# Projection results that ScalarE makes: their stores move from the queue of the loads to ScalarE's own queue

## The chip, the cores and the metric

The kernel runs on one core of a Trainium2 chip. The metric is the device time of one execution in microseconds (us). A core has a matrix engine (PE, with PEld for its weight loads), VectorE (DVE), ScalarE (ACT), GpSimd (POOL) and SyncE (SP). Each engine runs its own list of instructions strictly in order. A DMA (a transfer between the chip's memory and on-chip memory) is issued by an instruction in the list of one engine. In this kernel, before the change, all of them are issued from SP.

## The reference, cut to what matters

One step of a one-layer hybrid decoder for 1024 prompt tokens and 8 sample tokens. The inputs are projected by `w_in` (1024 x 3224), the parts go through four mixers (S5, mLSTM, GLA, RWKV-7), the outputs are joined by `w_out`, and a gated feed-forward network follows.

```python
h = rmsnorm(x, norm_mix)
proj = (h @ w_in).astype(F32)
(u, mq, mk, mv, mi, mf, mo, gq, gk, gv, ga, gg, rcols) = _split(proj, IN_SIZES)
...
mix = jnp.concatenate([y_s5, y_ml, y_gla, y_rw], axis=-1) @ w_out
x = x + mix.astype(x.dtype)
h2 = rmsnorm(x, norm_ffn)
up = (h2 @ ffn_w_up).astype(F32)
...
x = x + ffn.astype(x.dtype)
```

## The kernel before

**Stages.** The 1032 tokens are cut in two segments, `SEGS`: tokens 0 to 511, and tokens 512 to 1031 with the samples. `build` runs: the projection of segment 0, `win(0)`; the mixers for the first quarters of the tokens, `go(SEQ0)`; the projection of segment 1, `win(1)`; `w_out` and the feed-forward network of segment 0; the remaining mixers, `go(SEQ1)`; then `w_out` and the feed-forward network of segment 1. This is the order in which the program is written. On the engines the stages lie over one another: mixer work of segment 0 runs among the projection of segment 1, and so on.

**A projection.** Weights come as 128x1024 tiles of 512 KB (`load_w`, L1121 to L1123): SP issues the load into `wr` (every third one into `p`), ACT rounds it to a high part (`wh`, L1122), POOL makes the low part (`wl`, L1123). `mm3` (L1140 to L1142) multiplies three times for one product: high by high, high by low, low by high. There are two forms of projection:

- `w_in_fm` gives 128 features by the tokens of the segment. For segment 0, VectorE multiplies the result by the row norm (L1221). For segment 1 the inputs are already normed (`hr` is a list and `None`), so ScalarE copies the result out of PSUM (L1220), in two chunks of 260 tokens. One store then writes the tile `t` to a scratch tensor in the chip's memory (L1222): `rcD`, `mlD` or `glD`.
- `w_in_tm` gives tokens by 256 features. ScalarE copies the result out in both segments (L1249), and a store for every 256 tokens (L1250) writes it to `uD`, `gvD` or `mvD`.

The mixers read these scratch tensors back (`rcD` at L144 and L146, `uD` at L778, `glD` at L330, L332 and L364, `mlD` at L509 and L514, `gvD` at L331, `mvD` at L512). So a store here is followed, sooner or later, by a load of the same data from the same queue. The tiles `t` come from a pool of five (`TB`).

**What sets the order.** Nothing is put in order by hand. The recording layer's scheduler places each engine's instructions by a simulated timeline and by priorities: weight and input loads with their splitting have one base number (`S`), the projections and the feed-forward network another (`E`), their matmuls a third (`G`), the mixers follow the program. The result is a fixed list for each engine. A change of one instruction's engine can therefore move others, on all engines.

**Waits.** Each instruction carries the semaphores that it waits for. DMAs that land add to one of eight semaphores, which are dealt out in turn over all DMAs (`DMAHW0` to `DMAHW7`, with a number behind, in the rows below). Before a DMA is issued, its engine waits until the DMA before it on the same semaphore, some eight DMAs earlier in the schedule, has landed. Other waits are for the engine that made the data or that still reads the buffer (`Activation`, `DVE`, `Pool`, `PE`).

Of the kernel before, what the change touches and what calls it, by code (L numbers as in the profile page):

```python
# [1109 lines left out]
def load_w(k,src,tags=None):  # L1110

    nc=k.nc; k.wn+=1
    if tags: r=k.wp.tile([128,1024],F32,tag="wr",name="wr",bufs=k.wb[0]); h,l=[k.ga.tile([128,1024],F32R,tag=n,name=n) for n in tags]
    elif k.w3 and k.wn%3==0: r,h,l=[k.ga.tile([128,1024],t,tag=n,name=n) for n,t in (('p0',F32),('p1',F32R),('p2',F32R))]
    else: r,h,l=[k.wp.tile([128,1024],t,tag=n,name=n,bufs=b) for n,t,b in zip(('wr','wh','wl'),(F32,F32R,F32R),k.wb)]
    shp=src.shape; n=int(np.prod(shp[1:]))
    def view(t):
        v=t[:,0:n]
        return v if len(shp)==2 else v.rearrange("p (a b)->p a b",a=shp[1]) if len(shp)==3 else v.rearrange("p (c a b)->p c a b",c=shp[1],a=shp[2])
    with k.pr('S'):  # L1120
        nc.sync.dma_start(out=view(r),in_=src)  # L1121
        nc.scalar.copy(h[:,0:n],r[:,0:n])  # L1122
        for c in range(0,n,256): nc.gpsimd.tensor_tensor(out=l[:,c:c+256],in0=r[:,c:c+256],in1=h[:,c:c+256].bitcast(F32),op=ALU.subtract)  # L1123
    return view(h),view(l)

def tt(k): return k.tp.tile([128,HW],F32,tag="t",name="t",bufs=k.tb)
def htile(k,i): return k.ga.tile([128,2,HW],F32R,tag="h%d"%i,name="h%d"%i)
def gps(k,tag=None): return k.psm.tile([128,512],F32,tag=tag,name=tag,bufs=1 if tag=="mc" else 2) if tag else k.psg.tile([128,512],F32,tag="g",name="g")
# [5 lines left out]
def mm3(k,out,w,hs,c0,c1):  # L1134

    T=k.nc.tensor; wh,wl=w; n=len(hs)
    with k.pr('G'):
        for i,h in enumerate(hs):
            a=h[:,0,c0:c1]; b=h[:,1,c0:c1]
            T.matmul(out,wh[:,i],a,start=i==0,stop=False)  # L1140
            T.matmul(out,wh[:,i],b,start=False,stop=False)  # L1141
            T.matmul(out,wl[:,i],a,start=False,stop=i==n-1)  # L1142

def chunks(N):
    return [(0,N)] if N<=512 else [(0,N//2),(N//2,N)]
# [64 lines left out]
def w_in_fm(k,hr,seg,idx,w=None,tag=None):  # L1210
    nc=k.nc; c0,c1=seg; N=c1-c0; hs,r=hr
    w=w or load_w(k,k.wfm[idx])
    dst,sc=k.fmdst[idx]
    e=tt(k); ps=[]
    for a,b in chunks(N):
        p=gps(k,tag); ps.append(p)
        mm3(k,p[:,0:b-a],w,hs,a,b)
    if r is not None: r=r.rstd()
    for (a,b),p in zip(chunks(N),ps):
        if r is None: nc.scalar.activation(out=e[:,a:b],in_=p[:,0:b-a],func=AF.Identity,scale=sc)  # L1220
        else: nc.vector.scalar_tensor_tensor(out=e[:,a:b],in0=p[:,0:b-a],scalar=sc,in1=r[:,a:b],op0=ALU.mult,op1=ALU.mult)  # L1221
    nc.sync.dma_start(out=dst[:,c0:c1],in_=e[:,0:N])  # L1222

def w_in_tm(k,hr,seg,which):

    nc=k.nc; T=nc.tensor; V=nc.vector; A=nc.scalar; c0,c1=seg; N=c1-c0; hs,r=hr
    src=dict(mv=k.wmv,gv=k.wgv,u=k.wu)[which]; dst=dict(mv=k.mvD,gv=k.gvD,u=k.uD)[which]
    n=N//128; m=N%128
    ps=[]; q=None
    for pi in range(2):  # L1230
        wh,wl=load_w(k,src[pi])
        with k.pr('G'):
            for i in range(n):
                if pi==0 and i%2==0: ps.append(gps(k))
                o=ps[i//2][:,i%2*256:i%2*256+256]
                for kk in range(4):
                    h=hs[pi*4+kk]; a=h[:,0,i*128:i*128+128]; b=h[:,1,i*128:i*128+128]
                    z=T.matmul(o,a,wh[:,kk],start=pi==0 and kk==0 and i%2==0,stop=False)  # L1238
                    if pi==0 and kk==0 and i%2: k.tc.keep_in_program_order(z)
                    T.matmul(o,a,wl[:,kk],start=False,stop=False)  # L1240
                    T.matmul(o,b,wh[:,kk],start=False,stop=pi==1 and kk==3 and i%2==1)  # L1241
            if m:
                if pi==0: q=gps(k)
                for kk in range(4):
                    for u,w in enumerate((wh,wl)):
                        T.matmul(q[0:32+m,0:256],k.hd[:,pi*4+kk],w[:,kk],start=pi==0 and kk==0 and u==0,stop=pi==1 and kk==3 and u==1)
    for i in range(0,n,2):
        e=tt(k)
        for u in range(2): A.activation(out=e[:,u*256:u*256+256],in_=ps[i//2][:,u*256:u*256+256],func=AF.Identity,scale=r.rT[:,i+u:i+u+1] if r else 1.0)  # L1249
        nc.sync.dma_start(out=dst[c0+i*128:c0+i*128+256].rearrange("(u p) f->p u f",p=128),in_=e[:,0:512].rearrange("p (u f)->p u f",u=2))  # L1250
    if m:
        e=tt(k)[0:m,0:256]
        A.copy(e,q[0:m,0:256])
        V.tensor_tensor(out=e,in0=e,in1=q[32:32+m,0:256],op=ALU.add)
        nc.sync.dma_start(out=dst[c0+n*128:c1],in_=e)
# [139 lines left out]
def build(ctx,tc,a):  # L1395
# [22 lines left out]
    def win(s):  # L1418
# [24 lines left out]
        for n,(kd,i) in enumerate(ORDER):  # L1443
            with k.pr('E'):
                if kd=='fm': w_in_fm(k,hr,SEGS[s],i,w.pop(0) if w else None,{3:'mb',4:'mb',5:'mc'}.get(n) if s==0 else None)
                elif kd=='tm': w_in_tm(k,hr,SEGS[s],i)
                else: w_in_g(k,hr,SEGS[s])
                if s==0 and n==0: m.tokens()
            if s==0 and n==10: setup()
# [110 lines left out]
```

## Time and profile before

| what | value |
|---|---|
| median of 3 runs | 1469.82 us (1467.22 to 1471.71) |
| the profiled execution's own time | 1476.86 us |
| its span, first to last instruction | 1475.1 us |
| busy ACT, DVE, POOL | 674.7, 896.6, 889.9 us |
| mean granted TensorE clock | 0.977 |
| bytes moved by DMA | 179.80 MB, mean 122 GB/s |
| mean busy share of the 16 DMA engines, hardware queue | 39.3% |

The span is what the trace covers; the execution's time is 1.8 us longer. The clock is the share of full speed that the throttle granted to the matrix engine. A wait is given as "engine line tile <- what ended the wait: us in total, times, longest us". In a table by stretches, the columns are the stretch, its length, then for each engine its busy us and its count of instructions, the granted clock, the busy share of the DMA engines and GB/s.

### The profile page before, as it was taken

The page shows a single profiled execution, that of the slowest core. Times are in us where ns is not written, and L with a number is a line of the kernel's source. Part 1 is how long each engine was busy: PE and PEld are TensorE (multiplying, and loading weights), DVE is VectorE, ACT ScalarE, POOL GpSimd, SP SyncE. Part 2 cuts the span into 40 slices and gives each one's busy share as a digit, 9 for nine tenths or more (in the row PEclk, how much of TensorE's full clock was granted, in tenths as well). Part 3 has the DMA queues.
Part 4 walks back from the last instruction along what each step waited for, and adds up shares of the span by engine and source line. Part 5 has one row for each costly group of instructions (what it writes and reads, how often), then busy time and mean ns, then how long its engine had stood idle before and what let it go on. Part 6 is the DMA issues. An engine that isn't in the chain of part 4 may idle for free.

```text
span 1475.1 us, 26769 instructions
## 1 busy us (share of the span) xinstructions
PE 1411.1 (96%) x10115; PEld 1238.0 (84%) x10115; DVE 896.6 (61%) x1979; ACT 674.7 (46%) x1129; POOL 889.9 (60%) x1154
## 2 busy tenths in 40 slices
PE   8779998999999989999899999999999999999997
PEld 6657787988999767777677778878999999999997
DVE  8988757768558956776946854544255434343434
ACT  6153353657366463756635435344442323232323
POOL 8556456546345554665644655855876757676764
PEclk9989998999999999999999999999999999999999
DMA  6455444652355523433224442353434232332332
GB/s 230 158 169 149 148 132 123 214 150 96 100 167 159 157 98 91 144 109 90 83 78 126 125 135 73 120 166 89 134 108 129 86 97 91 89 99 87 100 90 88
DMA packets 110266, 179.80 MB, mean 122 GB/s; under 512 B 33016, under 2 KB 67192, under 8 KB 110136
## 3 DMA queue, kind: packets, MB, share of 16 engines
q1 hardware_dynamic: 110136, 178.08, 39.3%
q8 instruction: 80, 1.31, 0.4%
q14 instruction: 50, 0.41, 0.1%
HBM read 148.10 MB, written 28.41 MB: 120 GB/s over the span
## 4 chain that ended last, share of the span: by engine, by line
PE 69%; DVE 18%; ACT 3%; DMA 3%; issue 3%; POOL 2%; SPq 0%; DVEq 0%; POOLq 0%; ACTq 0%
PE g L1140 18%; PE g L1141 18%; PE g L1142 18%; PE g L1241 1%; PE g L1240 1%; PE g L1238 1%; PE ma L214 1%; POOL wl L1123 1%; DVE h L1193 1%; PE mb L401 1%; DVE t L1318 1%; PE ma L294 1%; DVE t L1388 0%; DVE ma L248 0%; DVE b4c L734 0%
## 5 line engine op out<-in xcount | busy, mean ns | idle before, releaser
L1123 POOL TENSOR_TENSOR wl<-wr,wh 128x256 fp32r<-128x256 f32 x708 | 558.2, 819 | 296.5 <-ACT wh L1122 282.4
L1141 PE MATMUL g<-h,wh 128*128 128x260 f32 (+1 forms) x1536 | 492.6, 321 | 2.4 <-DVE h L1193 2.3
L1140 PE MATMUL g<-h,wh 128*128 128x260 f32 (+1 forms) x1536 | 492.3, 322 | 1.9 <-DVE p L1132 1.5
L1142 PE MATMUL g<-h,wl 128*128 128x260 f32 (+1 forms) x1536 | 491.1, 320 | 0.6 <-POOL wl L1123 0.6
L1122 ACT CAST wh<-wr 128x1024 fp32r<-128x1024 f32 x177 | 185.2, 1046 | 315.5 <-PE g L1141 167.0
L1141 PEld LDWEIGHTS g<-h,wh 128*128 128x128 f32 x1536 | 290.6, 189 | 28.3 <-DVE h L1193 5.8
L1140 PEld LDWEIGHTS g<-h,wh 128*128 128x128 f32 x1536 | 289.5, 189 | 26.2 <-DVE p L1132 2.6
L1142 PEld LDWEIGHTS g<-h,wl 128*128 128x128 f32 x1536 | 290.9, 189 | 22.3 <-issue 1.1
L1140 PE MATMUL g<-p,wh 128*128 128x260 f32 (+1 forms) x496 | 163.4, 329 | 6.8 <-DVE p L1132 3.8
L1141 PE MATMUL g<-p,wh 128*128 128x260 f32 (+1 forms) x496 | 162.3, 327 | 0.0
L1142 PE MATMUL g<-p,wl 128*128 128x260 f32 (+1 forms) x496 | 162.0, 327 | 0.0
L1140 PEld LDWEIGHTS g<-p,wh 128*128 128x128 f32 x496 | 94.5, 191 | 16.2 <-DVE p L1132 4.6
L1142 PEld LDWEIGHTS g<-p,wl 128*128 128x128 f32 x496 | 94.4, 190 | 8.4 <-issue 0.2
L1141 PEld LDWEIGHTS g<-p,wh 128*128 128x128 f32 x496 | 94.7, 191 | 7.7
L1123 POOL TENSOR_TENSOR p<-p,p 128x256 fp32r<-128x256 f32 x76 | 61.6, 840 | 41.8 <-ACT p L1122 39.8
L1306 DVE TENSOR_TENSOR xb<-xb,g 128x260 f32<-128x260 f32 x80 | 33.6, 423 | 59.0 <-PE g L1142 58.9
L1306 DVE TENSOR_TENSOR xa<-xa,g 128x512 f32<-128x512 f32 x48 | 32.8, 684 | 47.8 <-PE g L1142 47.7
L1328 DVE TENSOR_TENSOR t<-g,r 128x260 f32<-128x260 f32 x44 | 18.6, 424 | 55.5 <-PE g L1142 50.6
L1141 PE MATMUL g<-h,p 128*128 128x260 f32 (+1 forms) x144 | 48.9, 339 | 0.0
L1140 PE MATMUL g<-h,p 128*128 128x260 f32 (+1 forms) x144 | 48.6, 338 | 0.0
L1142 PE MATMUL g<-h,p 128*128 128x260 f32 (+1 forms) x144 | 48.6, 338 | 0.0
L1318 DVE SCALAR_TENSOR_TENSOR t<-g,vec,t 128x511 f32<-128x511 f32 (+1 forms) x44 | 32.6, 742 | 22.5 <-ACT t L1317 22.1
(726 smaller groups left out, 2644.4 us busy)
## 6 DMA issues: line engine op xcount, KB each, us to landing
wr<-in_wup_dram SPq DMA_DIRECT2D x88, 512.0 KB
wr<-in_wfm_dram SPq DMA_DIRECT2D x27, 512.0 KB
wr<-in_wdn_dram SPq DMA_DIRECT2D x22, 512.0 KB
wr<-in_wdl_dram SPq DMA_DIRECT2D x22, 512.0 KB
wr<-in_wout_dram SPq DMA_DIRECT2D x13, 512.0 KB
p<-in_wfm_dram SPq DMA_DIRECT2D x11, 512.0 KB
t<-in_xT_dram SPq DMA_DIRECT2D x16, 260.0 KB
b4c<-B8Td SPq DMA_DIRECT2D x6, 512.0 KB
```

What stands on the lines that cost most here:

```text
L214: T.matmul(pA[:,ci,j],KB[r0:r0+64,j,cc].rearrange("p a b->p (a b)"),KR[r0:r0+64,j,cc].rearrange("p a b->p (a b)"),start=True,stop=True)
L294: T.matmul(pd[:,j],KBt[:,cc,j*128:(j+1)*128],VU[:,cc,j*128:(j+1)*128],start=True,stop=True)
L401: T.matmul(pl[cq*64:cq*64+64,cc,j],x[:,s0:s0+64],xq[:,:,s0//2:s0//2+32],start=True,stop=True)
L1122: nc.scalar.copy(h[:,0:n],r[:,0:n])
L1123: for c in range(0,n,256): nc.gpsimd.tensor_tensor(out=l[:,c:c+256],in0=r[:,c:c+256],in1=h[:,c:c+256].bitcast(F32),op=ALU.subtract)
L1140: T.matmul(out,wh[:,i],a,start=i==0,stop=False)
L1141: T.matmul(out,wh[:,i],b,start=False,stop=False)
L1142: T.matmul(out,wl[:,i],a,start=False,stop=i==n-1)
L1193: k.nc.vector.scalar_tensor_tensor(out=h[:,1,0:N],in0=x,scalar=g,in1=h[:,0,0:N].bitcast(F32),op0=ALU.mult,op1=ALU.subtract)
L1306: V.tensor_tensor(out=x2[m][:,a:b],in0=x2[m][:,a:b],in1=p[:,0:b-a],op=ALU.add)
L1318: for o,n in ((1,'cw1'),(2,'cw0')): V.scalar_tensor_tensor(out=acc[:,o:N],in0=p[:,0:N-o],scalar=v1(k,n,j),in1=acc[:,o:N],op0=ALU.mult,op1= ...
L1328: for (a,b),p in zip(ch,pg): V.tensor_tensor(out=g[:,2+a:2+b],in0=p[:,0:b-a],in1=r[:,a:b],op=ALU.mult)
```

## The change

```diff
@@ w_in_fm
     for (a,b),p in zip(chunks(N),ps):
         if r is None: nc.scalar.activation(out=e[:,a:b],in_=p[:,0:b-a],func=AF.Identity,scale=sc)
         else: nc.vector.scalar_tensor_tensor(out=e[:,a:b],in0=p[:,0:b-a],scalar=sc,in1=r[:,a:b],op0=ALU.mult,op1=ALU.mult)
-    nc.sync.dma_start(out=dst[:,c0:c1],in_=e[:,0:N])
+    (nc.scalar if r is None else nc.sync).dma_start(out=dst[:,c0:c1],in_=e[:,0:N])
@@ w_in_tm
         for u in range(2): A.activation(out=e[:,u*256:u*256+256],in_=ps[i//2][:,u*256:u*256+256],func=AF.Identity,scale=r.rT[:,i+u:i+u+1] if r else 1.0)
-        nc.sync.dma_start(out=dst[c0+i*128:c0+i*128+256].rearrange("(u p) f->p u f",p=128),in_=e[:,0:512].rearrange("p (u f)->p u f",u=2))
+        nc.scalar.dma_start(out=dst[c0+i*128:c0+i*128+256].rearrange("(u p) f->p u f",p=128),in_=e[:,0:512].rearrange("p (u f)->p u f",u=2))
```

31 stores change their engine: the 19 of L1222 in segment 1 and the 12 of L1250, 6 in each segment. The 19 stores of L1222 in segment 0, which VectorE's results feed, and all other DMAs stay on SP.

The first place is the end of the `u` projection of segment 0. On ACT (lines with + are new), L1249 copies the result out, L1122 rounds the next weights, L151 begins the first RWKV mixer with the loaded `r_rc`:

```order
 L1122 CAST wh<-wr 128x1024
 L1249 ACTIVATE t<-g,rT 128x256 x2
+L1250 DMA uD<-t 128x2x256
 L1122 CAST p_1149<-p_1148 128x1024
 L1249 ACTIVATE t<-g,rT 128x256 x2
 L151 ACTIVATE ma<-r_rc,half 128x256 x2
 L1164 ACTIVATE xr<-xr 128x520
+L1250 DMA uD<-t 128x2x256
 L151 ACTIVATE ma<-r_rc,half 128x256 x2
 L107 CAST r_1799<-r_xc 32x256 x2
```

The second store now stands behind ACT instructions that wait for the load of `r_rc`. On SP, at the same place, both are gone from between the loads:

```order
 L144 DMA r_rc<-rcD 128x7x256
 L1205 DMA xr<-in_xT_dram 128x520
-L1250 DMA uD<-t 128x2x256
 L1121 DMA wr<-in_wgv_dram 128x1024
-L1250 DMA uD<-t 128x2x256
 L1121 DMA p_1281<-in_wgv_dram 128x1024
 L1205 DMA xr<-in_xT_dram 128x520
```

Nothing else changes there, on either engine. The second place is late in the projection of segment 1, where features of the mLSTM (`mlD`) are stored. SP before, with the semaphores that each waits for: L450 stores a GLA result, L514 loads gates for the mLSTM, L146 loads `r_rc`, L479 stores the mLSTM's running maxima `MD`.

```order
L450 DMA yD<-b2c 128x2x256 [waits DMAHW4_49,DVE_49]
L1121 DMA p_5200<-in_wmv_dram 128x1024 [waits Pool_49]
L514 DMA b2a<-mlD 128x2x256 [waits DMAHW6_49]
L1222 DMA mlD<-t 128x520 [waits DMAHW7_49,Activation_49]
L1121 DMA wr<-in_wfm_dram 128x1024 [waits DMAHW0_49,Pool_49]
L479 DMA MD<-b2b 4x256 [waits DVE_49]
```

SP now, at the same place:

```order
L450 DMA yD<-b2c 128x2x256 [waits DMAHW1_49,DVE_49]
L514 DMA b2a<-mlD 128x2x256 [waits DMAHW2_49]
L146 DMA r_rc<-rcD 128x7x257 [waits DMAHW4_49,PE_49]
L1121 DMA p_5200<-in_wmv_dram 128x1024 [waits DMAHW5_49,Activation_49,Pool_49]
L960 DMA d_xm<-glD 128x2x8 [waits DMAHW6_49,DMAHW3_49]
L479 DMA MD<-b2b 4x256 [waits DMAHW7_49,DVE_49]
```

And ACT now, around one of the stores that left SP here (L151, L336 and L523 belong to the RWKV, GLA and mLSTM mixers):

```order
L1122 CAST wh<-wr 128x1024 [waits DMAHW0_49,PE_49,Pool_49]
L1220 ACTIVATE t<-g 128x260 [waits PE_49]
L151 ACTIVATE ma<-r_rc,half 128x256 [waits Activation_49]
L336 CAST b2c<-b_8434 96x256 [waits DMAHW6_49,DMAHW5_49,DMAHW4_49]
L1222 DMA mlD<-t 128x520 [waits DMAHW7_49,Activation_49]
L523 ACTIVATE b4c<-b4c 128x1024 [waits DVE_49]
```

The wait for `DMAHW7` that the store carries is one for SP's store of `MD` at L479, which itself waits for VectorE. Of the 31 stores on ACT, 22 carry such a wait for an earlier DMA, and 17 of those DMAs are issued by SP. The third place is on PE, where the two lists first part, in the last projection of segment 0. L1140 to L1142 and L1241 are projection matmuls, L258, L426 and L429 belong to the RWKV and GLA mixers:

```order
 L1241 MATMUL g<-wh,h_212 128x256
 L1140 MATMUL g<-h_174,p_1693 128x512
+L1141 MATMUL g<-h_174,p_1693 128x512
+L1142 MATMUL g<-h_174,p_1694 128x512
 L258 MATMUL ma<-r_KB,r_rc 32x32 x16
 L426 MATMUL mb<-b2e,g_S 128x128
...
 L426 MATMUL mb<-b2e,g_S 128x128
 L429 MATMUL mb<-b4b,b2b 64x128 x2
-L1141 MATMUL g<-h_174,p_1693 128x512
-L1142 MATMUL g<-h_174,p_1694 128x512
```

Two projection matmuls pass a piece of mixer work. From here on mixer matmuls stand a few to some hundred projection matmuls away from where they stood, mostly earlier, until the mixers end. When PE comes to the norm of the first feed-forward network (L1172, the sum over `x` after `w_out` of segment 0), 909 of 1523 mixer matmuls were behind it before, and 913 are now.

## The prediction

> **What bounds the kernel now.** I read the page's busy times first, then a table by stretches, then PE's own waits.
>
> ```profile
> PE 1411.1 (96%) x10115; PEld 1238.0 (84%) x10115; DVE 896.6 (61%) x1979; ACT 674.7 (46%) x1129; POOL 889.9 (60%) x1154
> ```
>
> PE is busy for 1411.1 of 1475.1 us. Its work stays the same, so only the 64.0 us in which it is idle, and the time in which its clock is lowered, can change. The table by stretches says where these lie.
>
> ```profile
> core 0: us, PE busy (x) PEld busy (x) DVE busy (x) ACT busy (x) POOL busy (x), PEclk, DMA share, GB/s
> 0.00:60.00 60.00, 54.77 (x251) 43.38 (x251) 52.14 (x164) 26.42 (x41) 39.04 (x68) 1.00 0.60 201
> 60.00:100.00 40.00, 24.53 (x116) 19.70 (x117) 36.84 (x109) 14.31 (x28) 25.31 (x30) 0.80 0.55 178
> 100.00:250.00 150.00, 138.49 (x983) 117.06 (x984) 112.33 (x280) 69.87 (x119) 80.82 (x106) 0.94 0.47 139
> 250.00:500.00 250.00, 248.26 (x2245) 224.90 (x2244) 172.84 (x412) 145.10 (x285) 124.61 (x169) 1.00 0.48 146
> 500.00:560.00 60.00, 54.82 (x377) 41.81 (x375) 41.67 (x111) 34.55 (x56) 40.62 (x44) 0.94 0.35 106
> 560.00:760.00 200.00, 193.34 (x1194) 149.85 (x1195) 146.65 (x310) 111.53 (x189) 113.56 (x144) 0.97 0.35 107
> 760.00:1060.00 300.00, 294.47 (x1627) 241.58 (x1626) 155.48 (x290) 135.12 (x236) 186.97 (x220) 0.99 0.39 117
> 1060.00:1476.00 416.00, 402.43 (x3331) 399.66 (x3329) 178.67 (x309) 137.79 (x179) 278.97 (x376) 0.99 0.32 97
> ```
>
> Idle is the stretch less PE's busy time: 5.2, 15.5, 11.5, 1.7, 5.2, 6.7, 5.5 and 12.7 us (the last one cut at the span's end). The stretch that holds 25 of the 31 moved stores, 250 to 500 us, is the one in which PE has almost no idle time, at full clock. Its only wait there is this one, for a load:
>
> ```profile
> PE mb L373 <- DMA b4d<-glD: 1.7, 1, 1.7
> ```
>
> Now what the stores do to SP, by the waits of SP's list in 250 to 500 us, and their issue times by line:
>
> ```profile
> SPq L1222 <- ACT t L1220: 51.8, 15, 10.4
> SPq L1250 <- ACT t L1249: 7.6, 4, 2.8
> ```
>
> ```profile
> L1222 SPq DMA_DIRECT2D mlD<-t x12: 319/320/1319, 169.5 to 476.4; - x12
> ```
>
> ```profile
> L1250 SPq DMA_DIRECT2D uD<-t x4: 371/502/772, 81.2 to 321.2; - x4
> ```
>
> SP stood for 59.4 us behind stores whose data ACT had not yet made, and loads stood behind them. That is a real hold on SP. But PE waited 1.7 us in all this time, so the weights that were held up still came early enough.
>
> **The change, part by part.** I sum against the profiled execution, 1476.86 us (span 1475.1 and 1.8 around it). It is 7.0 us over the median of the runs, 1469.82, and I carry the difference that I find over to the median.
>
> *SP's relief, segment 1.* Removed: 19 issues of 0.32 us and 6 of about 0.5 us, 9 us of SP's time, and up to 59.4 us of holds. All of it lies beside PE's work. Between 0 and -1.7 us, since there is no other idle time to give back; I take 0, because the one wait is for a load of `b4d`, whose buffer another mixer must first leave, not for a place behind a store.
>
> *Segment 0, the `u` stores.* Here PE has its two longest stops:
>
> ```profile
> PE ma L112 <- DVE r L108: 8.8, 1, 8.8
> PE g L1240 <- POOL p L1123: 6.8, 1, 6.8
> ```
>
> The second one ends at 66 us, before any moved store. The first one follows the load of `r_rc`, which the two stores surround. The timeline of SP, then of ACT, then of DVE (start, us, engine, line, what; idle before it in brackets):
>
> ```profile
> 78.53 0.53 SPq L144 DMA_DIRECT2D r_rc<-rcD  x1
> 81.24 0.77 SPq L1250 DMA_DIRECT2D uD<-t  x1
> 82.58 0.63 SPq L1250 DMA_DIRECT2D uD<-t  x1
> ```
>
> ```profile
> 75.07 0.83 ACT L1249 ACTIVATE t<-g,rT 128x256 f32<-128x256 f32 x2
> 87.62 0.87 ACT L151 ACTIVATE ma<-r_rc,half 128x256 f32<-128x256 f32 x2 [10.04 <-DMA r_rc<-rcD]
> 88.97 0.46 ACT L151 ACTIVATE ma<-r_rc,half 128x256 f32<-128x256 f32 x1
> ```
>
> ```profile
> 89.18 1.26 DVE L632 CAST b2f<-s_qi 128x8 f32<-128x8 int32 x1
> 90.36 0.47 DVE L152 SCALAR_TENSOR_TENSOR r_xc<-r_rc,vec,ma 128x256 f32<-128x256 f32 x1
> 91.21 0.86 DVE L152 SCALAR_TENSOR_TENSOR r_xa<-r_rc,vec,ma 128x256 f32<-128x256 f32 x2
> ```
>
> The first store can now go out at 76 us, ahead of `r_rc`, and the second only after `r_rc` has landed. Its 256 KB at the 178 GB/s of this stretch are 1.5 us, so `r_rc` may land 1.5 us later, or up to 3 us earlier, with both stores (512 KB) out of its way. Neither reaches PE: ACT has its first L151 done at about 88.1 us, and DVE, busy with the S5 tables in its own order, takes the result at 90.36. That covers 2.2 us of delay, and holds back any gain. The second store's issue on ACT (0.37 to 0.77 us by SP's rows) comes before the L151 at 88.97, whose result DVE takes at 91.21, 1.8 us after it is ready: covered too. Between -0.5 and +1 us, taken as 0. What is late next is DVE, as it is now.
>
> *Segment 0, the `gv` stores.* The second of them stood on SP ahead of three loads of the GLA mixer, for the last of which PE waited:
>
> ```profile
> 140.18 0.39 SPq L1250 DMA_DIRECT2D gvD<-t  x1
> 140.67 1.70 SPq L364 DMA_DIRECT2D b4d<-glD  x1
> ```
>
> ```profile
> 150.52 0.66 PE L373 MATMUL mb<-b4d,b4a 128*64 128x128 f32 x2 [3.13 <-DMA b4a<-glD]
> ```
>
> Its place frees 0.49 us of SP, so this stop shrinks by about 0.5 us. On ACT the first `gv` store comes just before the copy L748, which frees the PSUM tile of L746, and PE waited for that copy once; that gives 0.4 to 0.5 us back. Sum 0, between -0.5 and +0.5. The two `mvD` stores stand between mixer instructions at about 200 us: 0, up to 1 us if the chain of the mixer takes both issues.
>
> *ACT, segment 1.* Added: 25 issues of which the trace shows none on ACT. The nearest rows are SP's, 0.32 to 0.77 us each, longest 1.32; together 8 to 19 us, on an ACT that is busy for 145.1 of 250 us. Each issue also waits until its own copy is done, and, in 22 of 31 cases, until an earlier DMA has landed. What is queued behind is mixer work and the rounding of weights. The cover is PE's stock: PSUM has three tiles for projections, of which two can wait for their copy. A chunk of 24 matmuls takes 2.8 us, by the late stretch where almost only such matmuls run, 50.00 / 422 = 0.118 us each:
>
> ```profile
> 1200.00:1250.00 50.00, 50.00 (x422) 50.00 (x421) 22.46 (x36) 16.62 (x21) 37.06 (x52) 1.00 0.29 88
> ```
>
> So ACT may be held for about 5.7 us before PE stands for want of a PSUM tile. A mixer's matmul that PE meets too early has no such cover. Bounds: 0, and the 5.2 us of idle that PE has at 500 to 560 us, where ACT has the same share of 58% and mixers stand close together. I take +1.0, near the lower end, as the row of this very stretch shows 1.7.
>
> The Trainium skill ("DMA: Bandwidth & Descriptors", section "Issuing engines are not separate DMA queues") says that DMAs issued by several engines run on the same 16 DMA engines and that issuing from more of them only saves the sequencer's issue time. By it SP would gain some 9 us of issue time, none of which PE waits for, and the sum would be 0 instead of +1.0; it says nothing of the waits that a store brings to ACT's list, which no run shows yet.
>
> *The new order.* Mixer matmuls move among projection matmuls, but as many of them as before (913 against 909) stand ahead of the one gap that projections cannot fill, from `w_out` to the feed-forward network near 545 us. The stops that a new order can remove or make are of this kind, from PE's waits in 500 to 760 us:
>
> ```profile
> PE ma L294 <- DVE r_KB L291: 3.1, 2, 1.8
> PE mb L534 <- DVE b4c L530: 2.0, 1, 2.0
> PE g L1140 <- DVE t L127: 1.3, 1, 1.3
> PE mb L401 <- DVE b4f L388: 1.3, 1, 1.3
> ```
>
> They come from chains between PE and DVE that are as long as before. Both stretches hold 11.9 us of idle, and 0.06 x 60 + 0.03 x 200 = 9.6 us for the lowered clock: 21.5 us. Half of that, 10.7 us, is my bound to either side; the order alone does not tell the sign, so I take 0.
>
> Sum: 0 + 0 + 0 + 1.0 + 0 = +1.0 us, 1477.9 for the profiled execution, 1470.8 for the median.
>
> **The rivals.** *Faster.* With SP free, loads for the mixers come earlier, the mixers run ahead, and stops after 500 us fall. For it: the 59.4 us of holds, and the schedule that puts mixers earlier. Against it: PE shows no wait for a load there beyond 1.7 us. It gives up to -10.7 us, 1459; its middle is 1464. The Trainium skill ("Perfetto Trace Analysis", section "DMA Optimizations") advises one engine for inputs and another for outputs; by that rule this change should gain, and the rows here show room on SP, not on PE.
>
> *Slower.* ACT takes over SP's holds. The store of `mlD` behind the wait for `MD` is the place. SP's rows:
>
> ```profile
> SPq L450 <- DVE b2c L449: 5.8, 1, 5.8
> SPq L479 <- DVE b L484: 12.6, 4, 5.4
> ```
>
> ```profile
> 415.62 0.43 SPq L514 DMA_DIRECT2D b2a<-mlD  x1
> 418.03 0.33 SPq L1222 DMA_DIRECT2D mlD<-t  x1
> ```
>
> L514 and the store were 2.4 us apart; now ACT must wait until what SP issues has landed. For a small landing I take the copy of `r_KB` in the chain that ended last:
>
> ```profile
> 324.64 2.28 DMA r_KB<-r_KB
> ```
>
> A hold of 5.8 us and this landing make 8.1 us; 5.7 us of it are covered, so one hold costs PE 2.4 us. It decides from 5.7 us on. Four of them, at L514, at L479 and at the two weight loads of `w_out` that later stores wait for, make 9.6 us: 1479.4. Against it: a DMA eight places earlier has mostly long been issued, so the price needs SP to be held at just these places.
>
> *It does not do what it says.* Since a load waits for the DMA eight places earlier, SP can stand again for a store on ACT's queue. Then SP gains nothing, and the time is that of my forecast.
>
> **How the numbers follow.** A measurement of this kernel tells some 0.3%, 4.4 us, from no change (the runs of before lie 4.5 us apart). No change: 0.43, with the third rival in it. Faster: 0.29. Slower: 0.28. I predict 1470.8 us. The range goes to both rivals' ends, 1459 and 1479, and 3 us further on the slow side, where a lowered clock would add to ACT's holds: 1459 to 1482.
>
> **What would show it.** PE's idle in 250 to 500 us stays below 4 us if I am right about ACT; above 7 us, with waits of PE for mixer tiles or for `t`, the slow rival holds. SP's waits for `t` of L1220 must be gone, and waits of SP for POOL or for DMAs grow in their place. ACT should show waits for DMAs ahead of L1222 of less than 5.7 us. The stop of L112 near 98 us stays within 1 us of 8.8. Idle and clock in 500 to 760 us tell the fast rival: below 6 us of idle it is right. I am wrong if PE's idle changes by more than 4 us in a stretch that I put at 0, above all if the new order makes a new stop of some us after 500 us.

## The result and the profile after

The changed kernel takes **1460.22 us** in the median of 4 runs (1456.17 to 1461.71), the kernel before 1469.82: ratio **0.994, interval 0.9918 to 0.9962**. Its profiled execution took 1461.71 us. That is 9.6 us less, inside the range, but on the faster side and not "no change".

The page's busy line, and the queue that is new on it:

```profile
PE 1409.1 (97%) x10115; PEld 1238.2 (85%) x10115; DVE 895.7 (61%) x1979; ACT 674.6 (46%) x1129; POOL 895.8 (61%) x1154
q10 hardware_dynamic: 6000, 8.21, 1.6%
```

The work is the same; 8.21 MB now go by ACT's queue. The table by stretches of the changed kernel:

```profile
core 0: us, PE busy (x) PEld busy (x) DVE busy (x) ACT busy (x) POOL busy (x), PEclk, DMA share, GB/s
...
100.00:250.00 150.00, 142.29 (x1024) 120.76 (x1022) 114.13 (x284) 70.64 (x120) 82.85 (x111) 0.94 0.46 141
250.00:500.00 250.00, 248.63 (x2224) 224.63 (x2222) 176.34 (x426) 146.41 (x285) 120.90 (x163) 0.99 0.50 147
500.00:560.00 60.00, 56.20 (x379) 44.64 (x378) 40.47 (x101) 32.50 (x53) 42.81 (x44) 0.94 0.32 97
560.00:760.00 200.00, 197.47 (x1242) 152.38 (x1242) 152.47 (x323) 122.84 (x207) 122.25 (x153) 1.00 0.38 114
```

PE's idle from 250 to 500 us, where 25 of the 31 stores lay before (24 now, the first of them goes out at 246 us), is 1.4 us (1.7 before). From 560 to 760 us, where none lies, it falls from 6.7 to 2.5 us, and the clock rises from 0.97 to 1.00. PE's waits there are now these two:

```profile
PE g L1140 <- DVE p L1132: 1.6, 1, 1.6
PE mb L401 <- DVE r L247: 0.8, 1, 0.8
```

SP's waits from 250 to 500 us:

```profile
SPq L1121 <- POOL wl L1123: 22.2, 10, 4.3
SPq L1121 <- ACT p L1122: 21.8, 4, 9.8
SPq L1121 <- POOL p L1123: 15.2, 6, 5.4
...
SPq L461 <- DVE b2f L97: 9.3, 1, 9.3
SPq L509 <- DVE r L247: 7.4, 1, 7.4
SPq L332 <- DMA yD<-b2a: 5.9, 1, 5.9
```

The 59.4 us for `t` are gone. SP now waits more for weight buffers that ACT still reads (L1121 for L1122 of `p`: 21.8 us, 14.1 in the same list of before), and in new places for mixers and for a store that has to land. On ACT each of the 31 issues starts at most 0.03 us after the end of ACT's work ahead of it, so none waits, and each takes 0.33 us (L1222) or 0.37 to 0.38 us (L1250) in the median:

```profile
L1222 ACTq DMA_DIRECT2D rcD<-t x7: 326/326/338, 246.1 to 295.8; - x7
```

```profile
L1250 ACTq DMA_DIRECT2D uD<-t x4: 373/377/399, 75.9 to 321.2; - x4
```

The first trace of before is 7 us slower than its median, so a second one was taken (`before_again`, 1468.32 us), and the comparison below goes by it. PE's waits of it from 700 to 750 us:

```profile
PE mb L401 <- DVE b4f L388: 1.3, 1, 1.3
PE g L1140 <- DVE p L1132: 1.1, 1, 1.1
PE mb L401 <- DVE ma L248: 0.9, 1, 0.9
PE mb L393 <- DVE b4c L376: 0.5, 1, 0.5
PE mb L401 <- ACT r_xa L255: 0.4, 1, 0.4
```

and the row of that stretch, then the row of the same stretch in the changed kernel:

```profile
700.00:750.00 50.00, 45.85 (x341) 35.72 (x341) 40.08 (x80) 26.49 (x43) 28.61 (x35) 0.93 0.26 78
```

```profile
700.00:750.00 50.00, 50.00 (x353) 39.37 (x352) 34.46 (x90) 30.49 (x49) 27.89 (x36) 1.00 0.31 92
```

Five stops, 4.2 us, and a lowered clock are gone. VectorE's timeline shows what has moved there. It carries two chains here. One is the last GLA quarter's loop over seven levels (L377): VectorE, with one step on ScalarE, forms a level's operands (L384 to L388), PE multiplies them (L393 in the first level, L401 in the others), ScalarE takes the first result (L394), VectorE the others (L404, or L405 in the last five). The other is the 31 rounds of the last RWKV solve (L247, L248), ended by L249. Before (`before_again`):

```profile
719.78 0.71 DVE L249 STREAM_TRANSPOSE r<-ma 128x256 f32<-128x256 f32 x1
721.58 0.43 DVE L405 COPY_PREDICATED b4c<-lvm,mb 128x256 f32<-128x256 int32 x1
...
742.50 0.73 DVE L405 COPY_PREDICATED b4c<-lvm,mb 128x256 f32<-128x256 int32 x1
```

After:

```profile
698.46 0.44 DVE L405 COPY_PREDICATED b4c<-lvm,mb 128x256 f32<-128x256 int32 x1
...
716.45 0.73 DVE L405 COPY_PREDICATED b4c<-lvm,mb 128x256 f32<-128x256 int32 x1
719.20 0.73 DVE L249 STREAM_TRANSPOSE r<-ma 128x256 f32<-128x256 f32 x1
```

In the old list all of the solve stands ahead of the last five L405; in the new one, counted in VectorE's list, they stand among it, behind its rounds 13, 13, 19, 20 and 27. The last L405 comes 26 us earlier, while the solve ends at the same time. PE's list changed there too: between the later L401 groups the old list has matmuls of the RWKV mixer (L258, L263, L270) beside those of projections, the new one almost only those of projections. That the place among the solve is what takes the stops away is a reading of these lists; experiments 3 and 5 test it and speak against it as the whole reason.

### The profile page after: what moved, and what is told of

It is laid out like the page before. It is cut to its first block, busy times and chain, and to the rows that moved or that the text cites. A ratio compares the mean times of both kernels' runs of the same rounds, so it can differ in the third digit from the quotient of the medians.

```text
span 1459.9 us, 26765 instructions
## 1 busy us (share of the span) xinstructions
PE 1409.1 (97%) x10115; PEld 1238.2 (85%) x10115; DVE 895.7 (61%) x1979; ACT 674.6 (46%) x1129; POOL 895.8 (61%) x1154
## 3 DMA queue, kind: packets, MB, share of 16 engines
q10 hardware_dynamic: 6000, 8.21, 1.6%
## 4 chain that ended last, share of the span: by engine, by line
PE 46%; DVE 4%; POOL 1%; DMA 1%; issue 1%; ACT 0%; SPq 0%; DVEq 0%; POOLq 0%; ACTq 0%
PE g L1140 14%; PE g L1141 14%; PE g L1142 14%; POOL wl L1123 1%; DVE t L1388 0%; DVE yo L1369 0%; DVE t L1318 0%; DMA wr<-in_wdn_dram 0%; DVE h L1193 0%; PE g L1172 0%; DMA DV<-r_KB 0%; DMA DB<-d_o 0%; POOL t L1339 0%; DVE r_xa L977 0%; PE ma L290 0%
## 5 line engine op out<-in xcount | busy, mean ns | idle before, releaser
L1123 POOL TENSOR_TENSOR wl<-wr,wh 128x256 fp32r<-128x256 f32 x708 | 562.3, 825 | 274.8 <-ACT wh L1122 260.4
L1140 PE MATMUL g<-h,wh 128*128 128x260 f32 (+1 forms) x1536 | 492.6, 322 | 3.0 <-ACT h L1192 1.7
L1142 PE MATMUL g<-h,wl 128*128 128x260 f32 (+1 forms) x1536 | 490.6, 320 | 0.6 <-POOL wl L1123 0.6
L1122 ACT CAST wh<-wr 128x1024 fp32r<-128x1024 f32 x177 | 185.3, 1047 | 288.5 <-PE g L1141 157.1
L1140 PEld LDWEIGHTS g<-h,wh 128*128 128x128 f32 x1536 | 290.3, 189 | 27.1 <-ACT h L1192 2.1
L1142 PEld LDWEIGHTS g<-h,wl 128*128 128x128 f32 x1536 | 291.4, 190 | 22.3 <-POOL wl L1123 1.4
L1140 PE MATMUL g<-p,wh 128*128 128x260 f32 (+1 forms) x496 | 161.3, 325 | 4.1 <-DVE t L1340 1.7
L1141 PE MATMUL g<-p,wh 128*128 128x260 f32 (+1 forms) x496 | 160.9, 324 | 0.0
L1142 PE MATMUL g<-p,wl 128*128 128x260 f32 (+1 forms) x496 | 160.5, 324 | 0.0
L1140 PEld LDWEIGHTS g<-p,wh 128*128 128x128 f32 x496 | 93.3, 188 | 12.9 <-DVE t L1340 1.9
L1142 PEld LDWEIGHTS g<-p,wl 128*128 128x128 f32 x496 | 93.3, 188 | 8.8 <-issue 1.0
L1123 POOL TENSOR_TENSOR p<-p,p 128x256 fp32r<-128x256 f32 x76 | 61.7, 841 | 52.6 <-ACT p L1122 41.2
L1142 PE MATMUL g<-h,p 128*128 128x260 f32 (+1 forms) x144 | 48.8, 339 | 0.0
L1140 PE MATMUL g<-h,p 128*128 128x260 f32 (+1 forms) x144 | 48.4, 336 | 0.0
L1340 DVE TENSOR_TENSOR t<-t,g 128x260 f32<-128x260 f32 x44 | 16.7, 422 | 48.3 <-POOL t L1339 48.3
```

What stands on the lines that cost most here:

```text
L1340: for (a,b),q in zip(ch,pv): V.tensor_tensor(out=acc[:,a:b],in0=acc[:,a:b],in1=q[:,0:b-a],op=ALU.mult)
```

## The experiments

**How they were made.** The change alters two things at once, the queue and the order of every engine's list. To part them, a kernel is given the order of another one by edges between neighbours of each list, which fix the order of issue and add no wait; the moved stores alone stay free. "Old" and "new" order below are those of the kernel before and of the changed one.

```diff
+def hold_order(tc):
+    by={i.name:i for i in tc.nc.cur_bb.bb.instructions}
+    how=mybir.DependencyInfo(mybir.DependencyClass.NoSync,mybir.DependencyReason.DATA)
+    for e,first,*steps in json.loads(zlib.decompress(base64.b85decode(ORDERZ))):
+        last=first
+        for s in steps:
+            tc.add_manual_dep(by["I-%d"%(last+s)],"I-%d"%last,how,reason="held order"); last+=s
...
     build(ctx, tc, args)
+    hold_order(tc)
```

The table gives all of them. The last four columns are worked out from each one's trace. Each matmul gets a nominal duration, the median distance to the next start over all traces for matmuls of the same line and shape; the loss of a stretch is its time less the nominal durations in it. Stretches are cut by PE's work done, so that they hold the same part of the work in each kernel: A, about 218 to 513 us (segment 1's projection); B, to 570 us (from `w_out` to the feed-forward network); C, about 668 to 769 us (last GLA quarter). The scan is the last L349 on VectorE.

| kernel | moved stores on ACT | order | median us (runs) | ratio, interval | A | B | C | scan |
|---|---|---|---|---|---|---|---|---|
| before_again | none | old | 1468.32 (1) | | 25.5 | 13.6 | 10.8 | 1.21 |
| queue_only | all | old | 1468.15 (12) | 0.9995, 0.9983 to 1.0008 | 26.0 | 13.6 | 7.8 | 1.21 |
| order_only | none | new | 1464.33 (7) | 0.9963, 0.9948 to 0.9979 | 30.2 | 11.2 | 9.5 | 4.12 |
| order_only_2 | none | new | 1462.28 (12) | 0.9955, 0.9934 to 0.9975 | 31.3 | 11.0 | 3.7 | 1.22 |
| after | all | new | 1460.22 (4) | 0.994, 0.9918 to 0.9962 | 28.8 | 10.8 | 3.7 | 1.23 |
| after_again | all | new | 1459.0 (4) | 0.993, 0.9914 to 0.9946 | 26.6 | 9.9 | 3.7 | 1.23 |
| after_3 | all | new | 1459.81 (6) | 0.993, 0.9906 to 0.9954 | 28.6 | 10.4 | 3.7 | 1.22 |
| early_new | all | new to 555 us | 1465.25 (11) | 0.9972, 0.9953 to 0.9992 | 26.4 | 10.8 | 9.6 | 1.21 |
| late_5000 | none | new from 462 us | 1465.72 (12) | 0.9975, 0.9955 to 0.9996 | 27.6 | 12.5 | 3.5 | 1.23 |
| late_5500 | none | new from 503 us | 1466.91 (12) | 0.9989, 0.9969 to 1.001 | 26.0 | 16.9 | 7.5 | 4.15 |
| late_new | none | new from 555 us | 1470.51 (11) | 1.0025, 1.0006 to 1.0045 | 24.9 | 13.6 | 7.3 | 4.11 |
| late_6700 | none | new from 630 us | 1467.44 (12) | 0.9994, 0.9979 to 1.0008 | 25.3 | 13.6 | 10.8 | 1.21 |
| l1250_alone | 12 of L1250 | a third | 1468.1 (11) | 0.9996, 0.9983 to 1.0009 | 31.9 | 15.0 | 4.3 | 1.21 |
| l1222_alone | 19 of L1222 | almost new | 1463.8 (11) | 0.9969, 0.995 to 0.9988 | 25.3 | 10.5 | 8.0 | 4.14 |
| l1250_held | 12 of L1250 | new | 1461.26 (12) | 0.9952, 0.9937 to 0.9967 | 30.5 | 11.3 | 3.7 | 1.22 |
| l1222_held | 19 of L1222 | new | 1463.98 (12) | 0.9955, 0.9935 to 0.9975 | 26.8 | 10.7 | 7.5 | 4.17 |
| order_guard | none | new, two waits more | 1462.26 (10) | 0.9958, 0.9939 to 0.9978 | 29.3 | 11.0 | 6.4 | 1.23 |
| after_guard | all | new, two waits more | 1462.68 (11) | 0.9959, 0.9943 to 0.9976 | 28.6 | 10.2 | 5.0 | 1.23 |
| after_collide | all | new, two waits reversed | 1465.23 (12) | 0.9973, 0.9955 to 0.9991 | 28.5 | 10.5 | 8.3 | 1.23, 3 us late |

Single runs of one kernel lie far apart, 1456.69 to 1469.96 for order_only_2, so medians and ratios are read for the whole and the columns for the place. The columns are of the one execution that was traced, and its time can lie far from the median: 1457.30 us for l1222_alone, the fastest of its eleven, with the long scan, and 1466.80 us for order_only_2 with the short one. So a column tells what one stretch of one execution lost, and not why the median is what it is.

**1. Queue or order.** `queue_only`: the changed kernel with the old order.

> The 31 stores are issued from ScalarE, and every other instruction on every engine keeps the place that it had before the change. Theory Q (the queue itself pays: SyncE no longer holds up loads): 1458 to 1463 us, as the changed kernel. Theory O (the new order of the other instructions pays): 1467 to 1472 us, as before. If only the stop of TensorE for the load of b4a near 150 us is the queue's, and the rest is the order's: about 1466 us (4 us less than before).

`order_only`: the kernel before with the new order. `before_again` and `after_again` are the two kernels themselves.

> All stores stay on SyncE, and every other instruction on every engine stands where the changed kernel has it. Theory Q: 1467 us or more, since the loads stand behind the stores again. Theory O: 1458 to 1463 us. If the order pays only because SyncE is free (the early mixers would then wait for their loads): above 1472 us.

> The kernel before, unchanged, for a second trace. All theories: 1467 to 1472 us. If the stops of TensorE near 150, 545, 735 and 760 to 900 us are in this trace too, the differences between the two kernels there are not an accident of one execution.

> The changed kernel, unchanged, for a second trace and a longer comparison. All theories: 1456 to 1463 us, ratio 0.992 to 0.996; its milestones (how far TensorE is behind or ahead of the kernel before at equal work) within 2 us of the first trace's.

The queue alone gains nothing. The order alone, with every store on SP, gains 0.4%; its 1464.33 us lie between theory O's 1463 and theory Q's 1467. Both together gain 0.7% beside them. `queue_only` has the same five stops between 700 and 750 us as `before_again`, to the tenth, at a clock of 1.00 instead of 0.93, which makes its C 3 us lower:

```profile
700.00:750.00 50.00, 45.83 (x370) 35.84 (x369) 40.78 (x84) 25.25 (x41) 28.53 (x35) 1.00 0.26 80
```

**2. Where the order pays.** The two orders are joined at a seam: up to it the instructions stand as in one kernel's program, behind it as in the other's.

> Queues as before. Order of before up to the gap between w_out and the feed-forward network of segment 0 (about 555 us), order of the changed kernel from there on. Theory 'late order' (the gain of the order is made where the last GLA quarter meets the last RWKV solve): the five stops of PE between 706 and 746 us go (4.2 us, and the clock there rises from 0.91 to 1.00), the time falls by about 7 us to 1461 to 1463, ratio 0.994 to 0.996, with no store moved. Rival 'joint' (the gain needs mixers that are ahead already in segment 1, by a free SP): the stops come back in another place and the time stays within 2 us of before, 1467 to 1470.

> All 31 stores on ACT's queue. Order of the changed kernel up to about 555 us, order of before from there on. Theory 'late order': the five stops between 706 and 746 us stay, and what is left is segment 1 (0 to +2 us) and the bubble near 545 us (-2 us): 1466 to 1469, ratio 0.998 to 1.000. Rival 'relief' (SP's relief pays in the early part, and gives the second half of the gain): 1463 to 1465, ratio 0.996 to 0.997.

The theory of the late order fell. `early_new`, which still has the five stops, gains 0.28%, between the two expectations; its gain shows in B, 10.8 for 13.6. `late_new` loses. Its five stops are gone, but three others stand there (2.8 us, L401 and L393), and behind the seam, at 590 to 660 us, PE waits for the low part of a projection's input (L1132) and for pieces of the S5 mixer:

```profile
PE g L1140 <- DVE p L1132: 2.8, 1, 2.8
PE mb L829 <- issue: 1.6, 1, 1.6
PE mb L835 <- ACT b4b L832: 1.3, 1, 1.3
PE mb L790 <- ACT b4b L786: 1.2, 1, 1.2
```

**3. Each half of the diff by itself,** with the order that the scheduler then gives.

> Only the second half of the change: the 12 stores of L1250 on ACT's queue, the 19 of L1222 on SP's; the schedule comes out as it will (a third order). In it all of the last RWKV solve still stands ahead of the last five L405 on VectorE, as before. Theory 'late order': the stops near 706 to 746 us stay, 1466 to 1472, ratio 0.998 to 1.002. Rival 'relief by the L1250 stores': 1463 to 1466, ratio 0.996 to 0.998.

> Only the first half of the change: the 19 stores of L1222 on ACT's queue, the 12 of L1250 on SP's. The order comes out almost as that of the changed kernel (82 places of 8891 on PE differ), the last five L405 on VectorE at rounds 13 to 27 of the last RWKV solve. Theory 'late order' with the stores of L1222 as the hold on SP: as the whole change, 1458 to 1461, ratio 0.993 to 0.995. Rival (the L1250 stores give the second half): 1463 to 1465, ratio 0.996 to 0.997.

The L1250 half gives a third order and no gain, as expected, but not for the reason given: its C is 4.3, so the stops that were to stay are gone, and A and B, 6 and 1 us above `before_again`, take it back. Its trace has all of the solve ahead of the last five L405, as the old order has (L249 at 698.9 us, the L405 from 724.3 to 741.7 us), and yet PE has no stop from 660 to 770 us. Its PE list is another too: much of what stands between the L401 there is RWKV work (L282 to L302). So the place of the L405 among the solve is not needed to be rid of the stops. The L1222 half gives almost the new order and 0.31%, the rival's figure, with an A below and a B like the changed kernel's, and a C that is 4 us worse.

**4. A collision of GpSimd with VectorE.** `order_only`, `late_new` and `l1222_alone` share a scan of 4.1 us. VectorE's scan in `order_only`, then GpSimd beside it:

```profile
682.22 4.12 DVE L349 TENSOR_TENSOR_SCAN b2d<-m,b2c 128x512 f32<-128x512 bf16 x1
```

```profile
681.37 1.10 POOL L363 MEMSET b4d<- 64x512 f32 x2
682.44 2.81 POOL L1123 TENSOR_TENSOR wl<-wr,wh 128x256 fp32r<-128x256 f32 x4
```

The scan ends 1.1 us after the four L1123, about its own duration. Two waits were added to keep it off, in `order_guard` (stores on SP) and in `after_guard` (stores on ACT):

```diff
+    for late,early in (("I-6396","I-9960"),("I-6481","I-9975")):
+        tc.add_manual_dep(by[late],early,mybir.DependencyInfo(mybir.DependencyClass.Sync,mybir.DependencyReason.DATA),reason="L1123 behind L337 and L349")
```

> Queues as before, order of the changed kernel, and two waits more: the four L1123 of one weight on GpSimd wait for VectorE's L337, those of another for VectorE's scan L349 (both near 660 to 685 us). In the profiles of order_only, late_new and l1222_alone L349 took 4.1 us and L337 2.5 us, each beside such a train of L1123; in those of the changed kernel 1.23 and 0.49. Theory 'port' (GpSimd's train holds VectorE up, about 5 us, and this is what order_only lacks to the changed kernel): L349 1.2 to 1.7, L337 below 0.7, the stops at L401 fall from 4.2 to below 1 us, 1459 to 1461, ratio 0.993 to 0.995. Rival 'queue' (SP's own holds cost it): the two durations fall, the time stays at 1463 to 1466, ratio 0.996 to 0.998.

> The changed kernel, its order held, with the same two waits. Theory 'port': they cost nothing and where some runs of the changed kernel met the long scan they gain: 1456 to 1460, ratio 0.991 to 0.994. Rival: the held-up L1123 make weights late, 1461 to 1464.

The scan falls to 1.23 us in both. `order_guard` comes out between the two theories, at 1462.26, and `after_guard` at 1462.68, as its rival had it: the waits hold the L1123 back, and a stop of 2.0 us at L401 for L247 stays (0.8 in the changed kernel). What the pair shows is the equality: same order, same scan, and with the 31 stores on one queue or the other the medians differ by 0.4 us, which runs that spread over 6 to 7 us can't tell from nothing.

> Order of the changed kernel held, only the 12 stores of L1250 on ACT's queue, the 19 of L1222 on SP's. Theory 'port': the time goes with the scan, 1459 to 1461 where L349 takes 1.2 us, 1463 to 1466 where it takes 4.1. Rival 'queue' with the L1250 stores as what holds SP: 1459 to 1461 whatever the scan takes; with the L1222 stores: 1463 to 1466 whatever it takes.

`l1250_held` has the short scan and 1461.26, next to what both theories had for it. It tells little between them.

**5. The seam moved.**

> Queues as before, order of before up to about 630 us (L337 and L349 are in it), order of the changed kernel from there on; the last five L405 stand at rounds 22 to 27 of the last RWKV solve on VectorE. Theory 'late order': the five stops of PE between 706 and 746 us (4.2 us) go and nothing takes their place: 1462 to 1465, ratio 0.995 to 0.997. Rival 'fit' (an order pays only behind the state it was made from): new stops near the seam at 630 to 680 us eat it, 1467 to 1471, ratio 0.999 to 1.002.

The rival's time holds (1467.44), but not its place: nothing new stands at 630 to 680 us. The last L405 stand among the solve, at rounds 22 to 27, and other stops, near 702 to 711 us, take the place of the five:

```profile
PE mb L401 <- DVE b4e L388: 4.6, 2, 2.4
PE mb L393 <- DVE b4c L376: 1.2, 1, 1.2
```

With the third experiment this parts the stops from the place of the L405: in `late_6700` they stand among the solve and PE has 6.0 us of stops, in `l1250_alone` they stand behind it and PE has none. Which part of the lists decides stays open.

**6. The collision's price, and the order once more.** `after_collide` turns the two waits round; `order_only_2` and `after_3` are order_only and the changed kernel again, on one chip; `l1222_held` moves the L1222 stores alone, in the new order.

```diff
+    for late,early in (("I-9960","I-6399"),("I-9975","I-6484")):
```

> The changed kernel, its order held, with two waits the other way round: VectorE's L337 waits for the four L1123 beside it on GpSimd, the scan L349 for the other four. Theory 'port': L337 comes about 2 us and L349 about 3 us later than in the changed kernel, as in order_only, the stops at L401 come to about 4 us, and the time to that of order_only, 1463 to 1466 (ratio 0.996 to 0.998). Rival (the collision is hidden, the second half of the gain is something else): as the changed kernel beside it, 1458 to 1461.

> order_only once more, to stand beside the changed kernel on one chip: queues as before, order of the changed kernel. Theory 'port': long scan (4.1 us) and 1463 to 1466. Rival (the first time was a slow draw of seven runs): 1459 to 1461.

> Order of the changed kernel held, only the 19 stores of L1222 on ACT's queue. Theory 'port': 1463 to 1466 with a scan of 4.1 us, 1459 to 1462 with one of 1.2 us. Theory 'relief' (SP's holds by the L1222 stores in segment 1 cost the new order 2 to 3 us): 1459 to 1462 whatever the scan takes, and a loss between 220 and 516 us that is 3 us below that of order_only_2.

> The changed kernel itself, as measure for the three beside it: scan of 1.2 us, 1458 to 1461, ratio 0.993 to 0.995 by both theories; above 1462 the second half of its gain was a draw of few runs.

`after_collide` does what the port theory says: 1465.23 beside 1459.81. But `order_only_2` fits neither expectation: 1462.28, and this time its scan is short:

```profile
681.91 1.22 DVE L349 TENSOR_TENSOR_SCAN b2d<-m,b2c 128x512 f32<-128x512 bf16 x1
```

```profile
680.47 1.10 POOL L363 MEMSET b4d<- 64x512 f32 x2
682.22 3.54 POOL L1123 TENSOR_TENSOR wl<-wr,wh 128x256 fp32r<-128x256 f32 x4 [0.65 <-ACT wh L1122]
```

So the same program meets the collision in one execution and not in another. `l1222_held` has the long scan and the time that the port theory gives for it, 1463.98; its loss in A, 26.8, is 4.5 below that of order_only_2, as the relief theory had it. Its ratio is order_only_2's, 0.9955, so that the time of the whole decides for neither.

**7. The seam ahead of the bubble.**

> Queues as before, order of before up to about 462 us, order of the changed kernel from there on, so that segment 1 keeps the old order (where the new one loses 2 to 5 us more) and the bubble near 545 us and all behind it the new one. Theory 'place' (the order gains 3 us in the bubble and 7 us at 680 to 750 us, and each is there with the order of its place): stops at L294 near 545 us gone, no stop at L401 beyond 2.0, 1458 to 1462, ratio 0.992 to 0.995, with no store moved. Rival 'fit' (an order pays only behind the state that it was made from): new stops behind the seam, 1465 to 1470, ratio 0.997 to 1.001.

> The same with the seam at about 503 us, just ahead of the bubble. Theory 'place': as late_5000. Rival 'fit': stops at L294 as before (3 us) and a new stop at 620 to 640 us as in late_new, 1468 to 1472, ratio 0.999 to 1.003.

`late_5500` keeps the old stops in the bubble, meets the collision, and gains nothing that can be told. `late_5000` has the gain in C and a third of that in B in its profiled run (3.5 and 12.5, and 1459.66 us), but its median of 12 runs is 1465.72 (1457.86 to 1471.48): the place theory by its stops, the rival's time by its median. Why its runs lie so far apart stays open. No version beats the changed kernel.

## Why the prediction was wrong

**The step that failed** is the fifth: "*The new order.* [...] the order alone does not tell the sign, so I take 0." Its premise, "They come from chains between PE and DVE that are as long as before", does not carry this: each chain has its instructions as before, but what stands between its links on VectorE and on PE changed, and with it the stops. The order alone, put at 0, measured 0.9963 and 0.9955, some 6 us. That it changed on VectorE can be read off the two lists without a run, and only PE's list was shown; its sign can't, as the wrong expectation for `l1250_alone` shows. By the table, from `before_again` to the mean of the three changed runs: C -7.1 us, B -3.2, A +2.5. These three make -7.8 of the 8.5 us between those traced executions (1468.32 and 1459.86 in the mean), within the bound of 10.7 that was put on this step; about 3 of the 7.1 are the clock, which is 0.93 in the old order's stretch in `before` and `before_again` and 1.00 in `queue_only`. In B two stops at L294 go and one at L290 comes; `before_again`, then the changed kernel:

```profile
PE ma L294 <- DVE r_KB L291: 3.6, 2, 1.8
```

```profile
PE ma L290 <- DVE r_rs L287: 3.1, 1, 3.1
```

With the small ones that is 4.4 against 3.7 us of stops from 505 to 585 us. The clock there, 0.94 and 0.96, makes 1.6 us more; the rest of the 3.2 is not traced to a row.

**SP's relief was put at 0, and is 0 in the old order** (`queue_only`, 0.9995). The argument, that PE waited only 1.7 us, was right for that order: the wait at L373 for `b4d` is 1.7 us in `queue_only` too. In the new one A is 29.3 to 31.3 in the four profiles with the L1222 stores on SP, and 26.6 to 28.8 in the six with them on ACT, 2.3 us between the means. With them on SP, PE has stops of the mLSTM in A that the changed kernel has not; in `order_only_2`, from 218 to 520 us:

```profile
PE mb L534 <- DVE b4c L530: 0.8, 1, 0.8
PE mb L529 <- DVE b4c L522: 0.5, 1, 0.5
PE mb L548 <- DVE b4c L530: 0.5, 1, 0.5
```

`order_only` has 1.9 us of these three, `l1250_held` 1.0, but `order_guard` none, with an A of 29.3. That loads held behind the stores make these mixers late is argued, not shown. The new order costs segment 1 4.8 us (30.3 against 25.5), and a free SP gives about half of them back. The rule of the Trainium skill by which this change should gain ("Perfetto Trace Analysis", section "DMA Optimizations") bought nothing by itself here.

**What stays open** is the rest. order_only has a median of 1462.9 over its 19 runs, the changed kernel 1459.6 over its 14. The order alone is thus 6 of 9.5 us. For the 3 us between them there are two candidates, the 2.3 us in A, and the collision, which showed in none of the changed kernel's three profiles and in one of order_only's two. The pair with the guards speaks against the first, and with one or two profiles a kernel nothing is known of how often the collision falls. `after_collide` shows that the collision can cost this much: 1465.23 beside 1459.81. Nor is it sure that there are 3 us to share out: the intervals of order_only and after_again, on one chip, lie apart, those of order_only_2 and after_3, on another, overlap. It is not settled.

**The faster rival** had the outcome (mixers run ahead, stops after 500 us fall; 1459 to 1464) and put it down to the wrong cause. It was SP's free time that was to bring it; it is the order.

**The slower rival and the term for ACT (+1.0)** did not come: no issue waits on ACT, and the 25 issues of segment 1 take 19 x 0.33 + 6 x 0.37 = 8.5 us, the lower end of the 8 to 19 estimated. The term is 0. The rival's price also rested on a row from another place: SP's 5.8 us at L450 lie behind 500 us, where no moved store is; from 400 to 480 us, around the store in question, its waits at L450 and L479 are these:

```profile
SPq L479 <- DVE b L484: 2.8, 1, 2.8
SPq L450 <- DVE b2d L469: 1.3, 1, 1.3
```

**The `u` and `gv` stores** were put at 0, and nothing in the runs speaks against it. The stop at L112 is 7.3 us, off by more than the 1 us allowed, but it is 7.6 in `before_again` and 8.6 in `after_again`: it changes from run to run. The 3.13 us stop at L373 of the first trace is absent from the changed kernel's waits, but also from `before_again`, and it is 3.5 us in `l1250_held`, where the `gv` stores are on ACT: it too changes from run to run.

**That it does not do what it says** was partly so: SP's waits for `t` went, and waits for weight buffers and mixers took part of their place, without PE seeing it. The waits for POOL, which were to grow, fell: from 27.9 + 17.3 to 22.2 + 15.2 us.

**The signs named:** idle below 4 us from 250 to 500 us held. The faster rival's sign, less than 6 us of idle from 500 to 760 us, came out at 3.8 + 2.5 = 6.3. "I am wrong if PE's idle changes by more than 4 us in a stretch that I put at 0" is met against the first trace, from 6.7 to 2.5 us, and not against `before_again`, which has 5.5.

## What to carry to other kernels

Where a scheduler lays out the lists, a one-word change is two changes, and the list can weigh more than the edit: hold the order fixed and measure each by itself before a gain is put down to the edit. Compare the order on every engine, and not on the busiest alone, but don't read the sign of a change off one feature of one list: here the most visible one, how two serial chains lie on VectorE, went with the gain in most kernels and failed in two. A good order is good behind its own beginning: pieces of it behind another beginning gave back part or all of what they won.

## What the runs showed of the hardware

GpSimd and VectorE held each other up. Where the scan stood 0.22 us ahead of GpSimd's first L1123, it waited for all four of the train and took 4.12 us; where it stood 0.31 us ahead, with GpSimd idle for 0.65 us before, it took 1.22 us and the train 3.54 instead of 2.81. In one program both were seen, with 9.5 and 3.7 us in C. The other profiles divide in the same way: with the long scan (five in all) it leads by 0.21 to 0.27 us and GpSimd comes to L1123 from its L363 without a gap; with the new order and the short scan (six, where no wait was added) it leads by 0.31 to 0.32 us and GpSimd was idle for about 0.65 us. Whether the lead or the gap decides, these profiles don't tell. The Trainium skill ("SBUF — State Buffer", section "SBUF: two separate sides") says that VectorE, with two inputs in SBUF, and GpSimd share a port pair as an exclusive lock, which the one that starts first keeps for its whole instruction. The traces agree that it is exclusive; they add that the loser waited for four instructions in a row, and that a start 0.22 us earlier in the trace did not win it, where GpSimd came without a gap from other work.

An issue of these stores on ACT's queue took 0.33 to 0.38 us in the median of each form; on SP it was 0.32 to 0.50. In the old order PE lost nothing by the move (`queue_only`, 0.9995).
